# Listing the DeltaNet gates and first head pair first, and moving one S5 mixer behind DeltaNet, in a two-layer hybrid backbone on one core

## The chip, the cores and the metric

The kernel runs as one program on one core of a Trainium2 chip. The metric is the device time of one execution in microseconds (us), lower is better. The core's engines each work through their own list of instructions in a fixed order: TensorE (PE in the profile; PEld is its weight load, PEq its sequencer), VectorE (DVE), ScalarE (ACT), GpSimd (POOL), and SyncE (SP, which here issues nearly all transfers). An instruction waits for what it needs, and all that stands behind it on its engine waits with it. TensorE's clock has two levels, 1.2 and 2.4 GHz; the profile gives the granted clock of a stretch as a share of the upper one.

## The reference, cut to what matters

A flow-matching backbone of two layers over 768 tokens of width 1024: 256 context tokens and 512 latent ones. Only the latent tokens come out at the end, so in the second layer several stages handle those 512 alone. Each layer:

```
h  = modulated RMSNorm(x)
z  = h @ w_in        # dn_qkv, dn_z, dn_a, dn_b | s5_u | da_q, da_k, da_v | gla_...
y0 = gated DeltaNet(dn_qkv, dn_z, dn_a, dn_b)   # 4 heads of 64, both directions, chunks of 64
y1 = S5(s5_u)                                   # diagonal state space, width 256, both directions
y2 = differential attention(da_...)             # 4 heads
y3 = gated linear attention(gla_...)            # 4 heads
x  = x + w_out @ sum_i sigmoid(h @ w_gate_i + b_i) * (y_i @ w_branch_i)
x  = x + mixture of experts(modulated RMSNorm(x))    # 16 experts, top 2
```

DeltaNet cuts the tokens into chunks of 64; for each it solves a triangular system, and then carries a 64x64 state per head from chunk to chunk, one step after the other. `dn_a` and `dn_b` give its decay and its step size, the "gates" of this document's title; the sigmoids that weigh the four branches are called merge gates here.

## The kernel before, in words

Every large product runs as three matmuls of split operands: `wunit` loads a block of weights on SP, ScalarE makes the high part (L1318, L1315 with a scale), VectorE the low part (L1319, L1316), and `mm3` issues high x high, low x high and high x low on TensorE (L1328 to L1330). Blocks of weights pass through a small ring of buffers, so that the next loads wait until the splits before have read theirs.

In each layer `norm_a` writes the normalized tokens, and then one long function writes the four mixers in this order of the program text: projections, DeltaNet (`dn`, in the profile `dn_...`), gated linear attention (`gl_...`), differential attention (`da_...`), and the 32 blocks of merge gates (`pg`, L1735 to L1750), which need only the normalized tokens. `proj_cm` makes outputs with channels on the partitions (`pc`), `proj_tm` with tokens on them (`pt`). What a projection gives is stored to DRAM (`xd` for DeltaNet's q, k, v, `ud` for S5's input, `zd` for a gate of DeltaNet and also for a result within S5) and loaded again by its mixer.

A scheduler, not the text, sets the order on each engine: it walks the program with modelled durations and gives what is written earlier the preference. So the merge gates fill TensorE while the mixers wait. Pools bound this: DeltaNet's pool on the right side of SBUF is closed before S5's opens there when S5 follows, and DeltaNet's own has few buffers, so its second pair of heads runs behind its first. The pair loop stands at L1633; `dn_pair` is a generator that stops once, at `rq = next(pair)`, and is then run to its end. Names in the rows: `dn_n` norms of q and k, `dn_q`, `dn_u`, `dn_m`, `dn_b`, `dn_w`, `dn_o` the chunks' triangular solves and products, `dn_c` the state's steps (VectorE adds each to the state `Sh` at L640), `dn_s` the state's part of the outputs, `yT` the transposes of a mixer's result on its way to `yd`, `yst` the staged copy of it.

S5 (`s5_mix`) works in two halves of 128 channels: each loads tables (`td`, into `O`, `W`, `Tz`, `R`, `dec`) and its input `U` with a reversed copy `Ur`, makes `s_x` on TensorE, scans on VectorE, `s_y` on TensorE, and stores `z`; at the end `zT` and the weights `gw` are loaded, `s_g` makes a gate, and `ys` goes to `yd` (L1561). The tuple `S5E` says for each layer whether S5 is written ahead of DeltaNet or behind attention; before, the first layer has it behind and the second ahead, with its projection (columns from 1040) the first of all.

`merge` loads the four results from `yd` (`yr`, split into `yh`, `yl`), makes the branch products (`pb`), weighs and adds them on VectorE (L1787 to L1794), and multiplies by `w_out`, whose blocks are loaded through a ring of four.

Of the kernel before, what the change touches and what calls it, by code (L numbers as in the profile page):

```python
# [20 lines left out]
S5STEP = 4  # L21
NH = 4
DAST = 8
S5E = (0, 1)
AFTER = (1, 2, 5)
LP = (0, 0, 0)
PRP = (0, 0)
# [14 lines left out]
def const_blob():  # L42
# [21 lines left out]
    for n, a in parts.items():  # L64
# [11 lines left out]
PRO = {n: (sum(m for _, m in PRM[:i]), m) for i, (n, m) in enumerate(PRM)}  # L76
NPRM = sum(n for _, n in PRM)

WIN = ((1040, 256), (0, 256), (256, 256), (512, 256), (768, 272), (2832, 32), (2064, 256), (2320, 256), (2576, 256),
       (1552, 256), (1296, 256), (1808, 256))  # L80


def lay_out(x):
# [49 lines left out]
    o["wm"] = wm.reshape(2, 2, 4, 128, 24, 256).transpose(0, 4, 1, 3, 2, 5).reshape(2, 24, 2, 128, 1024)  # L133
    for c, n in WIN:
        o[f"win{c}"] = a["w_in"][:, :, c:c + n].reshape(2, 2, 4, 128, n).transpose(0, 1, 3, 2, 4).reshape(2, 2, 128, 4 * n)
# [209 lines left out]
def dn_conv(K, xp, m):  # L345


    nc, p, w = K.nc, K.dn, K.convw
    acc = p.tile([128, 772], F32, tag="s3", bufs=K.dn3, name="cacc")
    nc.scalar.activation(acc, xp[:, 0:772], AF.Copy, scale=w[:, 0, m:m + 1])  # L350
    for k in range(1, 5):
        nc.vector.scalar_tensor_tensor(acc, xp[:, k:k + 772], w[:, k, m:m + 1], acc, op0=OP.mult, op1=OP.add)
    th = p.tile([128, 772], F32, tag="s3", bufs=K.dn3, name="cth")
    nc.scalar.activation(th, acc, AF.Tanh, scale=0.5)
    nc.vector.scalar_tensor_tensor(acc, th, 1.0, acc, op0=OP.add, op1=OP.mult)
    return acc
# [294 lines left out]
def finish_heads(K, pool, tag, o, tiles, eps, gain, z=None, rq=None, sq=None, head=None):  # L651

    nc = K.nc
    t0, t1 = tiles
    n = (t1 - t0) * (o.shape[2] if head is None else 1)
    ov = o[:, t0:t1].rearrange("p t h e -> p (t h) e") if head is None else o[:, t0:t1, head]
    nc.scalar.activation(sq[:, 0:n, :], ov, AF.Square)
    ss = pool.tile([128, n], F32, tag=tag + "ss", name=tag + "ss")  # L660
    nc.vector.tensor_reduce(ss, sq[:, 0:n, :], axis=AX.X, op=OP.add)
    if rq is not None:
        rqv = rq[:, t0:t1].rearrange("p t h -> p (t h)")
        nc.vector.tensor_mul(ss, ss, rqv)
        nc.vector.tensor_mul(ss, ss, rqv)
    nc.vector.tensor_scalar(ss, ss, 1.0 / 64, eps, op0=OP.mult, op1=OP.add)
    r = rsqrt_(nc, pool, ss, [128, n], tag + "rs")
    if rq is not None:
        nc.vector.tensor_mul(r, r, rqv)
    nc.vector.tensor_mul(ov, ov, r[:, :, None].to_broadcast([128, n, 64]))  # L670
    gb = gain[:, None, :].to_broadcast([128, n, 64])
    if z is None:
        nc.vector.tensor_mul(ov, ov, gb)
        return
    zv = z[:, t0:t1].rearrange("p t (h e) -> p (t h) e", e=64)
    th = sq[:, 0:n, :]
    nc.scalar.activation(th, zv, AF.Tanh, scale=0.5)
    nc.vector.scalar_tensor_tensor(th, th, 1.0, zv, op0=OP.add, op1=OP.mult)
    nc.vector.tensor_mul(th, th, gb)
    nc.vector.tensor_mul(ov, ov, th)  # L680
# [642 lines left out]
def mm3(nc, out, terms, n=None):  # L1323


    n = n or len(terms)
    for i, (ah, al, bh, bl) in enumerate(terms):
        nc.tensor.matmul(out, ah, bh, start=(i == 0), stop=False)  # L1328
        nc.tensor.matmul(out, ah, bl, start=False, stop=False)  # L1329
        nc.tensor.matmul(out, al, bh, start=False, stop=(i == n - 1))  # L1330
# [120 lines left out]
def proj_units(K, ring, w, c0, n):  # L1451

    out = []
    for h in range(2):
        hi, lo = wunit(K, ring, K.I[f"win{c0}"][w, h].rearrange("p (k n) -> p k n", k=4), [128, 4, n], 3)
        out += [(hi[:, k], lo[:, k]) for k in range(4)]
    return out


def proj_cm(K, ring, w, ah, al, c0, n, parts, sink):  # L1460

    nc = K.nc
    u = proj_units(K, ring, w, c0, n)
    for m in range(0, n, 128):
        r = min(128, n - m)
        for s0, s1 in parts:
            ps = K.psd("pc")
            mm3(nc, ps[0:r, 0:s1 - s0], [(u[k][0][:, m:m + r], u[k][1][:, m:m + r], ah[:, k, s0:s1], al[:, k, s0:s1]) for k in range(8)])
            sink(m // 128, r, ps, (s0, s1))


def proj_tm(K, ring, w, ah, al, c0, n, tiles, sink):

    nc = K.nc
    u = proj_units(K, ring, w, c0, n)
    for t in tiles:
        ps = K.psd("pt")
        c = slice(t * 128, t * 128 + 128)
        mm3(nc, ps[:, 0:n], [(ah[:, k, c], al[:, k, c], u[k][0], u[k][1]) for k in range(8)])
        sink(t, ps)  # L1480


def put_yT(K, o, nch, tiles, yd, new, psm):

    nc = K.nc
    t0, t1 = tiles
    for j in range(nch):
        st = new([128, 768], "yst")
        a = t0
        while a < t1:  # L1490
            b = min(a + 4, t1)
            ps = psm("yT")
            for t in range(a, b):
                nc.tensor.transpose(ps[:, (t - a) * 128:(t - a + 1) * 128], o(t, j), K.c("id"))
            nc.scalar.activation(st[:, a * 128:b * 128], ps[:, 0:(b - a) * 128], AF.Copy)
            a = b
        nc.sync.dma_start(yd[j][:, t0 * 128:t1 * 128], st[:, t0 * 128:t1 * 128])
# [9 lines left out]
def s5_tds(K, l):  # L1507
    return [K.dram.tile([128, 7680], F32, name=f"td{l}{h}") for h in range(2)]


def mixers(K, l, md, hold, tile_of, yd, gd, tds):
# [7 lines left out]
    full = [(0, 256), (256, 768)]  # L1519
# [9 lines left out]
    ah = pa.tile([128, 8, T], F32R, name="ah")  # L1529
    al = pa.tile([128, 8, T], F32R, name="al")  # L1530
# [5 lines left out]
    w = l  # L1536
# [4 lines left out]
    ring = Hold(tc, f"pring{l}", "left")  # L1541
# [8 lines left out]
    def stage(shape, nm):  # L1550
        return ring.tile(shape, F32, tag="st" + str(shape[1]), bufs=2, name=nm)
# [11 lines left out]

    if S5E[l]:
        proj_cm(K, ring, w, ah, al, 1040, 256, full, sink_u)
# [4 lines left out]
    def sink_xd(base):  # L1570
        st = {}

        def f(m, r, ps, s):
            if s[0] == 0:
                st[0] = stage([128, 776], "xst")
                nc.gpsimd.memset(st[0][:, 0:2], 0.0)
                nc.gpsimd.memset(st[0][:, 258:262], 0.0)
                nc.gpsimd.memset(st[0][:, 774:776], 0.0)
            o = 2 if s[0] == 0 else 6
            nc.scalar.activation(st[0][:, s[0] + o:s[1] + o], ps[:, 0:s[1] - s[0]], AF.Copy)  # L1580
            if s[1] == T:
                nc.sync.dma_start(xd[m + base], st[0])
        return f

    for b in range(3):
        proj_cm(K, ring, w, ah, al, 256 * b, 256, full, sink_xd(2 * b))
    ab = gring.tile([128, NT, 16], F32, name="ab")

    def sink_z(t, ps):
# [4 lines left out]
            nc.sync.dma_start(zd[t * 128:(t + 1) * 128], st[:, 0:256])  # L1594

    proj_tm(K, ring, w, ah, al, 768, 272, range(NT), sink_z)
    if l == 0:
        st = Hold(tc, "s5t0", "right")
        tds = s5_tds(K, 0)
        for _ in s5_build(K, 0, st, K.psmb, tds, 4, 2):  # L1600
            pass
        st.close()
# [4 lines left out]
    if l == 0:  # L1607
# [3 lines left out]
        def some(n):  # L1611
            for _ in range(n):
                i, u = next(todo)
                mods(K, i, md[i], [u], pm, MB, K.psmb)
# [10 lines left out]
    def convs(pr):  # L1625
        tl = []
        for m in (pr, 2 + pr, 4 + pr):
            xp = dn.tile([128, 776], F32, tag="s3", bufs=K.dn3, name="xp")
            nc.sync.dma_start(xp, xd[m])
            tl.append(dn_conv(K, xp, m))  # L1630
        return tl

    for pr in range(2):  # L1633
        if pr and l == 0:
            some(MODS[1])
        ya = dn.tile([128, NT, 2, 64], F32, tag="ya", name="ya")
        pair = dn_pair(K, l, pr, S, *(tl if pr else convs(0)), ya, need)
        rq = next(pair)
        if pr == 0:
            tl = convs(1)  # L1640
        for _ in pair:
            pass
        zt = dn.tile([128, NT, 128], F32, tag="s3", bufs=K.dn3, name="zt")
        nc.sync.dma_start(zt[:, T0:], zd[T0 * 128:, 128 * pr:128 * pr + 128].rearrange("(t p) c -> p t c", p=128))
        finish_heads(K, dn, "fa", ya, (T0, NT), 1e-6, gain, zt, rq, sq=dn.tile([128, NT * 2, 64], F32, tag="s3", bufs=K.dn3, name="fsq"))
        put_yT(K, lambda t, j: ya[:, t].rearrange("p h e -> p (h e)"), 1, (T0, NT), yd[0, pr:pr + 1],
               lambda sh, n: dn.tile(sh, F32, tag="s3", bufs=K.dn3, name=n), K.psm)
# [21 lines left out]
    with tc.high_priority(PRP[l]):  # L1669
# [7 lines left out]
        proj_tm(K, ring, w, ah, al, 1808, 256, range(NT), sink_tm(vd, 0, 256))  # L1677
        if not S5E[l]:
            proj_cm(K, ring, w, ah, al, 1040, 256, full, sink_u)
# [51 lines left out]

    if not S5E[l]:
        s5()
# [770 lines left out]
```

## Time and profile before

| | |
|---|---|
| runs | 2712.81, 2721.1, 2722.15 us, median 2721.1 |
| profiled execution | 2708.16 us, its span 2706.4 us |
| TensorE busy, matmul | 2381.9 us, 88% of the span |
| TensorE busy, weight load | 1919.3 us, 71% |
| VectorE busy | 1894.2 us, 70% |
| ScalarE busy | 1228.0 us, 45% |
| GpSimd busy | 201.4 us, 7% |
| mean granted TensorE clock | 0.92 |

The shares are means over stages of different kinds: the mixers, where TensorE has projections and merge gates to fill it; the end of the mixers in each layer, where it has not; the merge; and the experts. Times in the rows are microseconds from the span's start. A busy time of a group of rows counts overlapping instructions once, while a mean duration is that of a single one, so that the count times the mean can exceed the busy time: matmuls are pipelined.

### The profile page before, as it was taken

The page shows a single profiled execution, that of the slowest core. Times are in us where ns is not written, and L with a number is a line of the kernel's source. Part 1 is how long each engine was busy: PE and PEld are TensorE (multiplying, and loading weights), DVE is VectorE, ACT ScalarE, POOL GpSimd, SP SyncE. Part 2 cuts the span into 40 slices and gives each one's busy share as a digit, 9 for nine tenths or more (in the row PEclk, how much of TensorE's full clock was granted, in tenths as well). Part 3 has the DMA queues.
Part 4 walks back from the last instruction along what each step waited for, and adds up shares of the span by engine and source line. Part 5 has one row for each costly group of instructions (what it writes and reads, how often), then busy time and mean ns, then how long its engine had stood idle before and what let it go on. Part 6 is the DMA issues. An engine that isn't in the chain of part 4 may idle for free. (4 is left out here: it accounts for less than half of the span.)

```text
span 2706.4 us, 46025 instructions
## 1 busy us (share of the span) xinstructions
PE 2381.9 (88%) x17551; PEld 1919.3 (71%) x17551; DVE 1894.2 (70%) x3917; ACT 1228.0 (45%) x1933; POOL 201.4 (7%) x220
## 2 busy tenths in 40 slices
PE   6999999999987894988989399999998877699993
PEld 4887668878865773776767288987786556588872
DVE  5857767864564957896778654677676586787785
ACT  4232233455533212655656332343666442476672
POOL 0000000000000000221221000000000000132210
PEclk8999999999986996999999699999997589799997
DMA  7488753431523764776778654443341085698884
GB/s 291 151 303 275 240 181 96 152 95 59 175 77 128 236 225 159 287 275 246 275 270 292 248 169 137 132 134 125 122 132 49 7 281 205 232 379 300 316 297 155
DMA packets 233719, 534.96 MB, mean 198 GB/s; under 512 B 86054, under 2 KB 116486, under 8 KB 207878
## 3 DMA queue, kind: packets, MB, share of 16 engines
q1 hardware_dynamic: 222534, 510.83, 55.2%
q0 software_dynamic: 10944, 20.99, 2.2%
q8 instruction: 142, 2.33, 0.3%
q14 instruction: 99, 0.81, 0.1%
HBM read 452.34 MB, written 100.35 MB: 204 GB/s over the span
## 5 line engine op out<-in xcount | busy, mean ns | idle before, releaser
L2228 DVE TENSOR_TENSOR lo<-raw,hi 128x2048 fp32r<-128x2048 f32 x192 | 437.8, 2289 | 87.7 <-ACT hi L2226 86.2
L2226 ACT ACTIVATE hi<-raw 128x2048 fp32r<-128x2048 f32 x192 | 364.6, 1914 | 100.5 <-PE pg L1330 71.8
L1328 PE MATMUL pg<-ah,wh 128*128 128x512 f32 (+1 forms) x768 | 280.2, 365 | 4.2 <-ACT gst L1748 4.0
L1330 PE MATMUL pg<-ah,wl 128*128 128x512 f32 (+1 forms) x768 | 280.0, 365 | 0.7 <-DVE wl L1319 0.7
L1329 PE MATMUL pg<-al,wh 128*128 128x512 f32 (+1 forms) x768 | 279.8, 364 | 0.0
L1329 PE MATMUL pg<-lo,xh 128*128 128x512 f32 x608 | 246.9, 407 | 12.6 <-DVE lo L2228 12.5
L1328 PE MATMUL pg<-hi,xh 128*128 128x512 f32 x608 | 243.9, 406 | 12.5 <-ACT hi L2226 11.9
L1319 DVE TENSOR_TENSOR wl<-wr,wh 128x512 fp32r<-128x512 f32 (+3 forms) x208 | 164.9, 795 | 118.9 <-ACT wh L1318 113.6
L1330 PE MATMUL pg<-hi,xl 128*128 128x512 f32 x608 | 244.1, 403 | 0.0
L1318 ACT ACTIVATE wh<-wr 128x512 fp32r<-128x512 f32 (+3 forms) x208 | 148.0, 715 | 211.4 <-PE pg L1329 83.7
L1328 PEld LDWEIGHTS pg<-ah,wh 128*128 128x128 f32 x768 | 147.5, 192 | 29.6 <-ACT gst L1748 5.0
L1330 PEld LDWEIGHTS pg<-ah,wl 128*128 128x128 f32 x768 | 147.4, 192 | 23.9 <-issue 1.9
L1329 PEld LDWEIGHTS pg<-al,wh 128*128 128x128 f32 x768 | 147.3, 192 | 22.1 <-issue 1.8
L1328 PE MATMUL pt<-wh,ah 128*128 128x256 f32 (+1 forms) x544 | 156.6, 289 | 2.1 <-ACT zst L1593 2.1
L1329 PE MATMUL pt<-wl,ah 128*128 128x256 f32 (+1 forms) x544 | 156.9, 289 | 0.0
L1330 PE MATMUL pt<-wh,al 128*128 128x256 f32 (+1 forms) x544 | 156.7, 288 | 0.0
L1329 PEld LDWEIGHTS pg<-lo,xh 128*128 128x128 f32 x608 | 117.6, 193 | 42.7 <-DVE lo L2228 19.0
L1328 PEld LDWEIGHTS pg<-hi,xh 128*128 128x128 f32 x608 | 116.9, 193 | 39.2 <-ACT hi L2226 14.7
L1330 PEld LDWEIGHTS pg<-hi,xl 128*128 128x128 f32 x608 | 117.1, 193 | 22.7
L1328 PE MATMUL pd<-hi,hh 128*128 128x512 f32 x304 | 120.1, 395 | 4.9 <-ACT hh L2280 4.9
L1328 PE MATMUL pc<-ah,wh 128*128 128x512 f32 (+3 forms) x352 | 120.4, 343 | 0.8 <-ACT ust L1556 0.7
L1329 PE MATMUL pc<-al,wh 128*128 128x256 f32 (+3 forms) x352 | 120.6, 343 | 0.0
(727 smaller groups left out, 5340.9 us busy)
## 6 DMA issues: line engine op xcount, KB each, us to landing
raw<-in_w_e_gate SPq DMA_DIRECT2D x64, 1024.0 KB
raw<-in_w_e_up SPq DMA_DIRECT2D x64, 1024.0 KB
raw<-in_w_e_down SPq DMA_DIRECT2D x64, 1024.0 KB
w<-in_wm SPq DMA_DIRECT2D x80, 512.0 KB
wr<-in_w_gate SPq DMA_DIRECT2D x128, 256.0 KB
wr<-in_win SPq DMA_DIRECT2D x40, 512.0 KB
gd<-gst SPq DMA_DIRECT2D x32, 384.0 KB
g<-gd SPq DMA_DIRECT2D x32, 384.0 KB
```

The lines of the kernel that those rows point to most:

```text
L1318: nc.scalar.activation(h, r, AF.Copy)
L1319: nc.vector.tensor_sub(l, r, h.bitcast(F32))
L1328: nc.tensor.matmul(out, ah, bh, start=(i == 0), stop=False)
L1329: nc.tensor.matmul(out, ah, bl, start=False, stop=False)
L1330: nc.tensor.matmul(out, al, bh, start=False, stop=(i == n - 1))
L2226: nc.scalar.activation(h, r, AF.Copy)
L2228: nc.vector.tensor_sub(l_, r, h.bitcast(F32))
```

## The change

Two things are changed. The tuple `S5E` puts the second layer's S5, with the projection of its input, behind DeltaNet and attention in the program text, as in the first layer. And among DeltaNet's projections the one with `dn_z`, `dn_a`, `dn_b` (columns 768 to 1040) comes first, followed by three blocks of 128 columns for the first pair of heads; the second pair's three blocks of 128 are written inside the pair loop, after the first pair's generator has stopped for the first time. Before, three blocks of 256 columns made q, k and v for both pairs at once, and `dn_z`, `dn_a`, `dn_b` followed. `WIN` lists the blocks in which the host lays out the weights. Both layers have the new order of projections.

```diff
-S5E = (0, 1)
+S5E = (0, 0)
...
-WIN = ((1040, 256), (0, 256), (256, 256), (512, 256), (768, 272), (2832, 32), (2064, 256), (2320, 256), (2576, 256),
+WIN = ((768, 272), (0, 128), (256, 128), (512, 128), (128, 128), (384, 128), (640, 128), (1040, 256), (2832, 32), (2064, 256), (2320, 256), (2576, 256),
        (1552, 256), (1296, 256), (1808, 256))
...
-    for b in range(3):
-        proj_cm(K, ring, w, ah, al, 256 * b, 256, full, sink_xd(2 * b))
+    def proj_pair(pr):
+        for b in range(3):
+            proj_cm(K, ring, w, ah, al, 256 * b + 128 * pr, 128, full, sink_xd(2 * b + pr))
+
     ab = gring.tile([128, NT, 16], F32, name="ab")
...
     proj_tm(K, ring, w, ah, al, 768, 272, range(NT), sink_z)
+    proj_pair(0)
     if l == 0:
...
         rq = next(pair)
         if pr == 0:
+            proj_pair(1)
             tl = convs(1)
```

The first place is the end of the second layer's mixers on TensorE, from the last merge-gate matmul on. This is the order before; `da_...` is attention, `dn_q` the start of the second pair's triangular solves.

```order
L1330 MATMUL pg<-ah,wl 128x512
L928 MATMUL da_o<-V,pe 64x64 x8
L864 MATMUL da_t<-idr,sp 96x128 x6
L918 MATMUL da_s<-st 128x512 x2
L864 MATMUL da_t<-idr,sp 96x128 x4
L918 MATMUL da_s<-st 128x512 x2
L864 MATMUL da_t<-idr,sp 96x128 x2
L928 MATMUL da_o<-V,pe 64x64 x8
L864 MATMUL da_t<-idr,sp 96x128 x4
L918 MATMUL da_s<-st 128x512 x2
L877 MATMUL da_m<-st 128x384
L508 MATMUL dn_q<-A,L 32x32
```

And this is the order of the changed kernel from its last merge-gate matmul on.

```order
L1330 MATMUL pg<-ah,wl 128x512
L877 MATMUL da_m<-st 128x384
L637 MATMUL dn_c<-Sh,Mt 64x64 x4
L877 MATMUL da_m<-st 128x384 x2
L928 MATMUL da_o<-V,pe 64x64 x8
L637 MATMUL dn_c<-Sh,Mt 64x64 x4
L877 MATMUL da_m<-st 128x384
L918 MATMUL da_s<-st 128x512
L637 MATMUL dn_c<-Sh,Mt 64x64 x4
L918 MATMUL da_s<-st 128x512
L637 MATMUL dn_c<-Sh,Mt 64x64 x2
L877 MATMUL da_m<-st 128x384
```

The second pair's solves moved ahead of the last merge gate; of its 40 state matmuls 28 stand behind it, four to a chunk. S5's first matmuls of the second layer follow them, among attention:

```order
L928 MATMUL da_o<-V,pe 64x64 x8
L877 MATMUL da_m<-st 128x384 x3
L928 MATMUL da_o<-V,pe 64x64 x8
L877 MATMUL da_m<-st 128x384
L918 MATMUL da_s<-st 128x512
L1198 MATMUL s_x<-U,W_22659 64x96 x12
L918 MATMUL da_s<-st 128x512
L1198 MATMUL s_x<-U,W_22659 64x96 x4
L877 MATMUL da_m<-st 128x384 x2
L1198 MATMUL s_x<-Ur,W_22661 64x96 x8
```

All of S5's matmuls in this layer now stand behind the last merge gate; before, all of them stood ahead of it, among the projections.

The second place is SP's list at the same end. Before, DeltaNet's and attention's last stores, the first six loads of `w_out` and the results' reloading for the merge:

```order
L1497 DMA yd_17483<-yst 128x512
L595 DMA EG<-gd 64x1024 x2
L1497 DMA yd_17483<-yst 128x512
L1310 DMA wr<-in_w_out 128x512 x4
L1497 DMA yd_17483<-yst 128x512
L1310 DMA wr<-in_w_out 128x512 x2
L1310 DMA yr<-yd_17483 128x512 x4
L1310 DMA wr<-in_w_branch 128x512 x2
```

In the changed kernel, from the first load of `w_out`, right behind attention's last store, to the same reloading:

```order
L1310 DMA wr<-in_w_out 128x512 x5
L1265 DMA zT<-zd 128x512
L1310 DMA wr<-in_w_out 128x512 x4
L1250 DMA zd<-z_22974 16x8x64 x8
L1310 DMA wr<-in_w_out 128x512 x2
L1265 DMA zT<-zd 128x512
L1267 DMA gw<-in_s_glu_w 128x2x256
L1310 DMA wr<-in_w_out 128x512 x5
L1561 DMA yd_17519<-ys_23095 128x512
L1561 DMA yd_17519<-ys_23107 128x512
L1310 DMA yr<-yd_17519 128x512 x4
L1310 DMA wr<-in_w_branch 128x512 x2
```

All sixteen loads of `w_out` moved ahead of S5's last stores and so of the merge; ten of them stood within the merge before.

## Rows read from the trace of the kernel before

**Rows 1.** Table by stretches: start:end, length, busy us (x instructions), clock, DMA share, GB/s.
```profile
core 0: us, PE busy (x) PEld busy (x) DVE busy (x) ACT busy (x) POOL busy (x), PEclk, DMA share, GB/s
...
791.00:857.00 66.00, 46.93 (x389) 31.97 (x388) 34.13 (x98) 17.80 (x38) 0.32 (x3) 0.61 0.14 41
1550.00:2041.00 491.00, 483.31 (x4095) 411.27 (x4093) 323.94 (x727) 213.20 (x405) 12.03 (x32) 0.99 0.44 133
2041.00:2166.00 125.00, 105.39 (x1211) 75.21 (x1210) 75.54 (x222) 66.27 (x158) 0.84 (x4) 0.63 0.11 28
...
2178.00:2234.00 56.00, 51.02 (x192) 35.40 (x192) 53.52 (x89) 22.18 (x36) 0.00 (x0) 0.97 0.83 277
```

**Rows 2.** Tiles dn_n and pg, TensorE, second layer: durations ns min/median/max, first, last start.
```profile
L382 PE MATMUL dn_n<-sq,cb x48: 272/273/297, 1715.1 to 1966.1; 128*32 128x128 f32 x48
...
L1330 PE MATMUL pg<-ah,wl x256: 387/389/632, 1779.2 to 2040.8; 128*128 128x512 f32 x128
```

**Rows 3.** Groups of TensorE, 1550 to 1690: S5's first and last of five.
```profile
L1239 PE MATMUL s_y<-X,O 64*64 64x64 f32 x256 | 10.9, 226 | 0.0
...
L1198 PE MATMUL s_x<-Ur,W 128*64 128x96 f32 x64 | 3.1, 249 | 0.0
```

**Rows 4.** The same view, 1690 to 1960, first pair: state matmuls; eight other groups' first, third, last.
```profile
L637 PE MATMUL dn_c<-Sh,Mt 64*64 64x64 f32 x80 | 6.0, 230 | 0.0
L540 PE MATMUL dn_u<-KR,Tt 64*64 64x64 f32 x96 | 3.8, 222 | 0.0
...
L568 PE MATMUL dn_m<-kd,W 64*64 64x64 f32 x80 | 3.3, 225 | 3.3 <-DVE Mt L570 3.3
...
L516 PE MATMUL dn_q<-Tt,Q 32*32 32x32 f32 x96 | 1.0, 193 | 0.0
```

**Rows 5.** Time line of VectorE, 2131 to 2167: first and last of ten state updates.
```profile
2133.13 0.60 DVE L640 TENSOR_TENSOR Sh<-Sh,dn_c 64x128 f32<-64x128 f32 x2
...
2153.90 0.59 DVE L640 TENSOR_TENSOR Sh<-Sh,dn_c 64x128 f32<-64x128 f32 x2
```

**Rows 6.** Time line of TensorE, 2164.5 to 2179: start, us, instruction, [idle before <-releaser].
```profile
2165.21 1.09 PE L1494 MATMUL yT<-cb,ya 128*128 128x128 f32 x4 [3.05 <-DVE ya L680]
2177.76 0.80 PE L1328 MATMUL pb<-yh,wh 128*128 128x512 f32 x1 [11.46 <-ACT wh L1318]
```

**Rows 7.** Time lines of TensorE: DeltaNet's last transposes, S5's halves, first and second layer.
```profile
712.35 0.82 PE L1494 MATMUL yT<-cb,ya 128*128 128x128 f32 x6
...
734.35 0.88 PE L1198 MATMUL s_x<-U,W 128*64 128x96 f32 x16
...
791.75 1.54 PE L1198 MATMUL s_x<-U,W 128*64 128x96 f32 x32
...
1595.74 0.96 PE L1198 MATMUL s_x<-U,W 128*64 128x96 f32 x18
...
1636.58 1.54 PE L1198 MATMUL s_x<-U,W 128*64 128x96 f32 x32 [0.52 <-DMA U<-ud]
```

**Rows 8.** Time lines of SP's queue: S5's stores in both layers, its first input load.
```profile
850.57 3.72 SPq L1561 DMA_DIRECT2D yd<-ys  x2
...
1581.22 0.46 SPq L1185 DMA_DIRECT2D U<-ud  x1
...
1684.41 0.32 SPq L1561 DMA_DIRECT2D yd<-ys  x1
```

**Rows 9.** Groups of VectorE, 2178 to 2234: the splits of w_out.
```profile
L1316 DVE SCALAR_TENSOR_TENSOR wl<-wr,wh 128x512 fp32r<-128x512 f32 x10 | 6.8, 696 | 0.0
```

**Rows 10.** Waits, 1550 to 2041: waited for, us in total, times, longest.
```profile
ACT wh L1318 <- DMA wr<-in_w_gate: 25.8, 10, 8.0
```

**Rows 11.** Groups of TensorE, 2041 to 2166.5: attention's matmuls on V and scores.
```profile
L918 PE MATMUL da_s<-st 98*128 98x512 f32 x34 | 20.4, 644 | 2.1 <-ACT st L865 1.7 <-ACT pe L921 0.4
...
L928 PE MATMUL da_o<-V,pe 128*64 128x64 f32 x288 | 17.5, 289 | 1.4 <-DVE pe L924 1.3
```

## The prediction

> **What bounds the kernel now.** I began with the table of stretches [rows 1], which cuts the second layer where its character changes. From 1550 to 2041 us TensorE is busy 483.3 of 491 us at full clock: there the kernel lasts as long as TensorE's queue, and no wait of another engine shows in the time. It ends with the last gate matmul: the row of the gate tile has its last start at 2040.8 [rows 2]. From 2041 to 2166 the same engine is busy 105 of 125 us at a granted clock of 0.63, between the levels 1.2 and 2.4 GHz: what is left there is a chain, DeltaNet's second pair of heads, with attention's remainder beside it. Third, the merge, 2178 to 2234: VectorE 53.5 and TensorE 51.0 of 56 us, so VectorE is just ahead.
>
> Who ends the tail is in the time lines: DeltaNet's ten state updates on VectorE run from 2133.13 to 2153.90 [rows 5], its normalized result is transposed at 2165.21, and the merge's first matmul starts 12.6 us later, at 2177.76, held by the split of a stored result [rows 6]. The second pair starts late because its first norm matmuls stand behind the first pair's: the norm tile's 48 matmuls run in two bursts, from 1715.1 and at 1966.1 [rows 2]. S5 of this layer was done long before, its last store issued at 1684.41 [rows 8].
>
> So the change is read as an exchange: S5's chain goes from a stretch that TensorE fills anyway to the end of the layer's chain, and DeltaNet's second pair goes the other way.
>
> **Term 1: TensorE's queue up to the last gate matmul, +5 us.** S5's five groups of matmuls leave it; busy times 10.9 to 3.1 us, sum 26.4 [rows 3]. By the order, all of the second pair but 28 of its 40 state matmuls now stands ahead of the last gate matmul. At full clock the first pair shows what that is worth: eight groups, 3.8 to 1.0 us, sum 21.6, and 12/40 of the state matmuls' 6.0, 1.8 [rows 4]. Of attention, 16 of 136 instructions on V and 6 of 34 score matmuls come ahead too: 16/136 x 17.5 + 6/34 x 20.4 = 5.7 us in the tail [rows 11], at full clock about 5.7 x 0.63 = 3.6. So 27.0 comes for 26.4. To this I add one wait of the size that the first pair has, 3.3 us on VectorE before `dn_m` [rows 4], and a microsecond for smaller ones. Bounds: 0, and +14 for four such waits.
>
> **Term 2: the tail, +17 us.** What stands behind the last gate matmul has four links, one after the other.
> The seven remaining state updates: ten took 20.8 us [rows 5], about 2.1 each, so 15 (13 for six intervals, 20 if they take as long as all ten).
> From the last update to the transposes of DeltaNet's result: 2165.21 - 2153.90 = 11.3 [rows 5, 6].
> From there to S5's first matmul: S5's buffers open only when DeltaNet's are closed, and its tables and `U` are loaded then. The first layer, which already has this order, shows it: 712.35 to 734.35, 22.0 us [rows 7]. The second layer of before shows 14.5 us from the issue of the first `U` (1581.22) to its first matmul (1595.74) [rows 7, 8], a floor. I take 20, since less is on the DMA queues in the tail than among the first layer's gate loads.
> S5 from its first matmul to its last store: 1684.41 - 1595.74 = 88.7 us at full clock, 120 in the first layer (734.35 to 850.57 + 3.72), where the second half ran at the tail clock [rows 7, 8]. The first half takes 40.8 before the second starts (1636.58), and the second 47.8 in the second layer, 62.5 in the first [rows 7, 8]. With attention beside it and no gates, I take 41 + 55 = 96.
> Sum 15 + 11 + 20 + 96 = 142; before, the same way is 2165.2 - 2041 = 124 to 125. The 12.6 us from there to the merge's first matmul stay: S5's store is loaded and split as DeltaNet's was. Bounds: 13 + 11 + 14.5 + 88.7 = 127 (+2) and 20 + 11 + 22 + 120 = 173 (+48).
>
> **Term 3: the merge, -4 us.** Ten splits of `w_out` lie in its first stage, 6.8 us of VectorE [rows 9]. In the new order they stand ahead of S5's last outputs, so they are done in the tail, beside a chain that leaves VectorE time (75.5 of 125 busy [rows 1]). TensorE's 51.0 is then next; of the 56 us about 4 can go. Bounds 0 (the splits delay S5's output by as much) and -6.8.
>
> **Term 4: projections and the first layer, 0.** Matmuls are the same in number and length; six loads and splits of 512 KB become twelve of 256 KB. They are hidden behind TensorE's queue: ScalarE waited 25.8 us, ten times, for gate weights of 256 KB [rows 10], in a stretch in which TensorE lost 7.7 us to everything [rows 1]. If the cover were gone, at the start of a layer's projections, each load would show its latency, some 2.6 us by that row. The earlier start of DeltaNet is nothing in itself, since the queue is what lasts. In the first layer the order barely changes but at one place: S5's second half stood right behind the last gate matmul (it started at 791.75 [rows 7]) and now some 45 gate matmuls stand behind its start, half of them of half length; at 0.39 us [rows 2] for the long ones that is up to 12 us of head start. But what feeds that half (tables, `U`) comes when it came before, so I take nothing. Bounds -12 and +8 (three loads uncovered).
>
> A rule speaks against the smaller loads. The Trainium skill, DMA: Bandwidth & Descriptors, section Bandwidth, asks for loads of 1 MiB and more, and gives 0.95 us for 64 KB and 6.15 for 1 MB; between these lines, an estimate, twelve loads of 256 KB are 23.9 us and six of 512 KB 20.3, +3.6 us a layer, which would make the time below about 7 us longer. No run here times one load by itself; the row of the gate weights lets me keep 0.
>
> **Sum.** 5 + 17 - 4 + 0 = +18 us on the profiled execution's own 2708.2, 2726. That execution lies 12.9 us under the median of the runs, 2721.1, so I forecast 2739 us. A measurement here can tell about 0.5%, 13.6 us, from no change.
>
> **The rivals.**
> No measurable change: every link of the tail at its floor, 127 us, because TensorE stays at the 2.4 GHz level, as it was in S5 of before. Then +2 +2 -4 = 0, up to +13: 2721 to 2734. For it: nothing of S5 needs more than the 88.7 shown. Against: the tail's clock was 0.63 with as many of attention's wide matmuls in it as there will be, and the first layer's S5 tail (791 to 857) has 0.61 [rows 1]. The halves can't run side by side to win it back: in TensorE's new order all of the first half's output matmuls stand ahead of the second half's first.
> Faster: the place is the first layer's S5. If its second half really starts 12 us before the last gate matmul, the 66 us of that layer's tail [rows 1] become 54. It decides only if the second layer's tail also stays at its floor: +2 +2 -4 -12 = -12, and with the whole 6.8 us of the merge -15, 2706 to 2709; any term of the second layer above its floor takes it back. For it: a queue that is freed there is worth its full length, since TensorE waits in that tail. Against: of the first layer's 57 us between the halves nothing shows TensorE's queue as the cause.
> Slower by more: on SP eleven `w_out` loads now stand between the first `zT` and S5's own stores; the ring has four buffers, each freed by a VectorE split, and what is queued behind a waiting load is S5's result, for which the merge waits. Six splits of 0.7 us and loads between them are some 8 us; with S5 at the first layer's 120 us the tail is 15 + 11 + 20 + 120 + 8 = 174, +49, and in all 2766 to 2775.
> The change may also leave DeltaNet where it was: if the second pair still ended last, the tail would hold both chains. The order excludes this, but not waits in the gates' stretch (Term 1's upper end).
>
> **Chances and range.** Forecast, slower by 0.5 to 1.5%: 0.39. Slower by more: 0.14. No measurable change: 0.31. Faster by over 0.5%, for this rival and what I don't see: 0.16. That makes 0.53 slower, 0.31 same, 0.16 faster. For 8 in 10 the range leaves out most of the faster case and half of the worst: 2704 to 2772. The likeliest case alone lies from 2735 to 2762.
>
> **What would show it.** The new profile should have: the last gate matmul within 0 to 14 us of 2041, measured from the layer's start; the first pair's norm matmuls some 90 us earlier and the second's over 100; the last state update some 15 us behind the last gate matmul, instead of 113; S5's first matmul some 46 us behind it; S5's last store as the last release before the merge; no `w_out` split among the merge's first products; the first layer's tail as long as before. I am wrong if S5 takes under 89 us in the tail, if the tail's clock is near 1, or if the gate stretch grows by more than 14 us because DeltaNet's waits now stand in TensorE's queue.

## The result, and the profile after

The changed kernel takes 2736.3 us in the median of four runs (2731.6 to 2739.3), the kernel before 2719.0; the ratio is 1.0065, 95% interval 1.0041 to 1.0089: slower, as forecast, by 17 us where 18 were worked out. Run again later it gave 1.0065 (1.0036 to 1.0095). The profiled execution took 2731.6 us, its span 2729.8, 23.4 more than that of before.

The table of stretches of the changed kernel (columns as in [rows 1]). The rows of the second layer are cut at the same events as before, but the second one, the tail, runs on to S5's last store; the first row's start, 781, is no event: it lies 4 us ahead of the start of S5's second half and 15 ahead of the first layer's last gate matmul.

```profile
core 0: us, PE busy (x) PEld busy (x) DVE busy (x) ACT busy (x) POOL busy (x), PEclk, DMA share, GB/s
...
781.00:848.00 67.00, 56.23 (x460) 40.37 (x459) 35.74 (x103) 21.05 (x48) 0.25 (x2) 0.70 0.19 56
1540.00:2044.00 504.00, 494.67 (x4406) 419.33 (x4406) 312.10 (x700) 225.23 (x432) 12.06 (x30) 0.98 0.39 114
2044.00:2197.00 153.00, 102.04 (x901) 74.18 (x899) 96.24 (x271) 65.75 (x155) 0.82 (x6) 0.55 0.33 102
...
2206.00:2256.00 50.00, 48.03 (x191) 36.31 (x189) 46.26 (x76) 15.37 (x25) 0.00 (x0) 0.95 0.76 242
```

Against [rows 1]: the stretch that TensorE fills is 504 instead of 491 us, the tail 153 instead of 125, and at a granted clock of 0.55 instead of 0.63; the merge's products are shorter, and there TensorE, with 48.0 of 50, is now ahead of VectorE.

The tiles `dn_n` and `pg` (answering to [rows 2]) show what moved: the second layer starts at 1539.9 now, 9.7 us earlier; relative to that the first pair's norms start 93 us earlier, and the second pair's last one starts 129 us earlier, while the last gate matmul comes 12.6 us later.

```profile
L382 PE MATMUL dn_n<-sq,cb x48: 272/273/297, 1612.4 to 1827.0; 128*32 128x128 f32 x48
...
L1330 PE MATMUL pg<-ah,wl x256: 387/389/796, 1770.5 to 2043.7; 128*128 128x512 f32 x128
```

The tail's chain on TensorE, from the time line (answering to [rows 6, 7]): DeltaNet's transposes, the starts of S5's two halves, S5's gate, and the merge's first product.

```profile
2072.70 1.09 PE L1494 MATMUL yT<-cb,ya 128*128 128x128 f32 x4 [8.68 <-DVE nx L895]
...
2092.11 2.19 PE L1198 MATMUL s_x<-U,W 128*64 128x96 f32 x24 [0.28 <-issue]
...
2143.84 2.51 PE L1198 MATMUL s_x<-U,W 128*64 128x96 f32 x28 [1.02 <-DMA U<-ud]
...
2188.38 6.20 PE L1277 MATMUL s_g<-zT,gw 128*128 128x256 f32 x16 [15.43 <-DMA gw<-in_s_glu_w]
2204.98 0.80 PE L1328 MATMUL pb<-yh,wh 128*128 128x512 f32 x1 [10.41 <-ACT wh L1318]
```

And the end of it on SP's queue (answering to [rows 8]): the loads of `w_out` stand between S5's `zT`, its second half's stores of `z`, `gw` and its own last stores.

```profile
2173.59 0.43 SPq L1265 DMA_DIRECT2D zT<-zd  x1
2174.57 3.59 SPq L1310 DMA_DIRECT2D wr<-in_w_out  x4
2178.21 3.81 SPq L1250 DMA_DIRECT2D zd<-z  x8
...
2183.86 0.43 SPq L1267 DMA_DIRECT2D gw<-in_s_glu_w  x1
2184.33 6.29 SPq L1310 DMA_DIRECT2D wr<-in_w_out  x5
2194.00 2.76 SPq L1561 DMA_DIRECT2D yd<-ys  x2
```

The span's 23.4 us are made up so: -9.7 up to the second layer's first norm matmul; +12.6 from there to the last gate matmul; +24.3 from that to the merge's first product (137.0 before, 161.3 now); -4.4 from there to its second product (56.2, 51.8); +0.6 after it.

### The profile page after: what moved, and what is told of

It reads as the page before. It is cut to its first block, busy times and chain, and to the rows that moved or that the text cites. A ratio compares the mean times of both kernels' runs of the same rounds, so it can differ in the third digit from the quotient of the medians.

```text
span 2729.8 us, 46084 instructions
## 1 busy us (share of the span) xinstructions
PE 2380.6 (87%) x17551; PEld 1925.5 (71%) x17551; DVE 1897.2 (69%) x3929; ACT 1231.1 (45%) x1945; POOL 196.2 (7%) x220
## 5 line engine op out<-in xcount | busy, mean ns | idle before, releaser
L1328 PE MATMUL pc<-ah,wh 128*128 128x256 f32 (+3 forms) x352 | 120.3, 343 | 2.2 <-ACT qst L1669 1.2
```

## The experiments

"S5 late" and "S5 early" mean the second layer's S5 behind or ahead of DeltaNet. The times of all kernels, with the ratio to the kernel before on the same chip. The kernels ran on several chips, so two medians of different rows can belong to different chips; the ratio, over all runs and with its interval, is the safer comparison. The last column is from one profile of each kernel.

| kernel | median us | ratio (95%) | from the second layer's start to its last gate matmul, to the merge's first product, to its second product |
|---|---|---|---|
| before | 2715 to 2719 | 1 | 491.2, 137.0, 56.2 |
| the change | 2736.3 | 1.0065 (1.0041 to 1.0089) | 503.8, 161.3, 51.8 |
| the change again | 2737.3 | 1.0065 (1.0036 to 1.0095) | 503.0, 162.4, 51.5 |
| S5 late alone | 2734.5 | 1.0072 (1.0045 to 1.0098) | 485.4, 172.3, 51.7 |
| projections alone | 2716.6 | 1.0005 (0.9978 to 1.0032) | 507.1, 142.0, 56.1 |
| gates first, whole blocks | 2692.9 | 0.9908 (0.9877 to 0.9939) | 500.5, 120.3, 63.0 |
| the same again | 2692.9 | 0.9909 (0.9875 to 0.9943) | 496.1, 119.1, 64.7 |
| gates first, whole, S5 late | 2715.1 | 0.9998 (0.9973 to 1.0022) | 500.4, 154.0, 50.7 |
| split in the second layer only | 2700.3 | 0.9932 (0.9909 to 0.9956) | 505.3, 120.3, 64.9 |
| split, all in front | 2734.8 | 1.0065 (1.0035 to 1.0095) | 497.1, 121.3, 62.4 |
| the change, `w_out` late | 2742.4 | 1.0092 (1.0058 to 1.0126) | 506.4, 156.3, 59.8 |
| the change, no attention | 2667.3 | 0.9826 (0.9759 to 0.9894) | 465.5, 138.2, 51.8 |
| the change, 6 gate blocks held | 2712.6 | 1.0005 (0.9975 to 1.0035) | see below |
| gates first, whole, S5 late, 6 held | 2699.9 | 0.9953 (0.9928 to 0.9977) | see below |

**S5 late alone.**

```diff
 # the kernel before
-S5E = (0, 1)
+S5E = (0, 0)
```

> The kernel before with S5E = (0, 0) alone: the second layer's S5 behind DeltaNet, projections as before. Theory (the two halves of the change act in different layers: the S5 move costs the second layer some 33 us between its start and its second product, the new projection order gives the first layer 9.7): first layer as before (S5's second half at 791 to 793, merge at 867 to 868), second layer slower than in the changed kernel, because more of the second pair (12 dn_b, all dn_w, dn_o and 40 dn_c instead of 28 dn_c) stands behind the last merge gate: 30 to 42 us over the kernel before, ratio 1.011 to 1.016. Rival (the new projections cost the second layer time, and the S5 move little): within 10 us of before, ratio under 1.004.

It is 17 us slower than before, as slow as the whole change. The rival falls, but the size of the theory does too, 30 to 42 us: the tail is longer than the change's, as expected (172.3), and the stretch ahead of it shorter (485.4), since there is less of the second pair in it. The merge, with the `w_out` splits out of it, gives 4.5 us back (51.7).

**Projections alone.**

```diff
 # the changed kernel
-S5E = (0, 0)
+S5E = (0, 1)
```

> The changed kernel with S5E = (0, 1): the new projection order in both layers, the second layer's S5 ahead of DeltaNet as before. Theory: the first layer keeps its 9 to 10 us, the second layer's end is as before (the order has the same second-pair instructions behind the last merge gate), so 5 to 13 us faster than before, ratio 0.995 to 0.998. Rival (the 12 smaller loads uncover latency in the second layer's start): second layer 5 us or more slower than before from its first norm matmul to its last merge gate, ratio 0.999 or more.

No change that can be measured. The first layer's merge starts at 856.1, 11.4 us earlier than before, so the theory's gain is there, but the second layer takes it back: 507.1 to the last gate matmul, and 142.0 behind it. The rival's number was met, but not its reason: in those 507.1 us TensorE is idle for 7.1, against 7.7 in [rows 1], so no load's latency shows there. What differs is the granted clock, 0.95 against 0.99.

**Gates first, whole blocks.**

```diff
 # the kernel before
-    for b in range(3):
-        proj_cm(K, ring, w, ah, al, 256 * b, 256, full, sink_xd(2 * b))
...
     proj_tm(K, ring, w, ah, al, 768, 272, range(NT), sink_z)
+    for b in range(3):
+        proj_cm(K, ring, w, ah, al, 256 * b, 256, full, sink_xd(2 * b))
```

> The kernel before with one thing changed: the projection of the gates (768 to 1040) ahead of the three blocks of 256, which stay whole. S5E as before. Theory (the first layer gains because DeltaNet starts some 5 us earlier and S5's second half comes to stand ahead of the last merge gates): the first layer's S5 store 6 to 10 us earlier, ratio 0.995 to 0.998. Rival (the gain comes from listing the second pair's blocks later): first layer within 3 us of before, ratio 0.999 to 1.001.

More than expected: 25 us faster than before, and the same in a second set of runs. Its second layer's tail has the same matmuls as that of projections alone, in another order. VectorE's time line shows it, first and last state update of the second pair, in projections alone (last gate matmul at 2045.6):

```profile
2140.64 0.60 DVE L640 TENSOR_TENSOR Sh<-Sh,dn_c 64x128 f32<-64x128 f32 x2
...
2163.14 0.59 DVE L640 TENSOR_TENSOR Sh<-Sh,dn_c 64x128 f32<-64x128 f32 x2 [0.69 <-PE dn_c L637]
```

and in the second profile of gates first (last gate matmul at 2039.2), where then TensorE's time line shows the end of the mixers:

```profile
2111.15 0.60 DVE L640 TENSOR_TENSOR Sh<-Sh,dn_c 64x128 f32<-64x128 f32 x2 [2.18 <-PE dn_c L637]
...
2127.47 0.29 DVE L640 TENSOR_TENSOR Sh<-Sh,dn_c 64x128 f32<-64x128 f32 x1
```

```profile
2144.05 1.05 PE L1494 MATMUL yT<-cb,ya 128*128 128x128 f32 x4
...
2157.59 1.09 PE L1494 MATMUL yT<-cb,o 128*128 128x128 f32 x4 [10.87 <-DVE o L673]
2158.32 0.78 PE L1328 MATMUL pb<-yh,wh 128*128 128x512 f32 x1
```

Here the scheduler put the last 28 state matmuls together, ahead of attention's remainder. DeltaNet's result is transposed 13 us before attention's last, the loads of five of the eight stored results are issued meanwhile, and its first product stands 0.7 us behind attention's transposes, where [rows 6] has 12.6 behind DeltaNet's. The merge then takes longer, 63 to 65 us, as its later inputs come in (the last three stored results are loaded from 2161.38 on); in all some 10 us are won from the last gate matmul to the second product (183 to 184 against 193.2).

**Gates first again.** The same kernel.

> The gates-first kernel once more, beside the others on one chip, for a second profile. Theory: 2688 to 2703, ratio 0.988 to 0.994; last merge gate to the merge's second product near 183 us, first layer's merge at 848 to 857. Rival (its gain was that chip's): ratio above 0.996.

It repeats: 183.8 us from the last gate matmul to the second product, the first layer's merge at 849.1.

**Gates first, whole blocks, S5 late.**

```diff
 # gates first, whole blocks
-S5E = (0, 1)
+S5E = (0, 0)
```

> The gates-first kernel (whole blocks of 256, gates ahead of them) with the second layer's S5 moved behind DeltaNet: the change without the splitting into pairs. Theory (the S5 move is what costs, by a longer chain behind the last merge gate, whatever the projection order): 18 to 30 us slower than the gates-first kernel (ratio 0.991 to the kernel before), so 2708 to 2724 us, ratio 0.998 to 1.003; last merge gate to the merge's first product 155 to 172 us. Rival (splitting the pairs is what costs, and the S5 move is cheap on this base): within 8 us of the gates-first kernel, ratio 0.989 to 0.994.

22 us slower than gates first with S5 early: the theory's band; the way to the merge's first product, 154.0, is just below its 155. So in the medians moving S5 costs 17 (old projections: 2734.5 against 2717.5), 20 (new ones: 2736.3 against 2716.6) or 22 us, on three bases; by the ratios it is 0.7, 0.6 and 0.9%, or 20, 16 and 24 us. With intervals of some 0.3% on each ratio the three do not differ.

**Split in the second layer only.**

```diff
 # projections alone
+    if l:
         proj_pair(0)
+    else:
+        for b in range(3):
+            proj_cm(K, ring, w, ah, al, 256 * b, 256, full, sink_xd(2 * b))
...
-            proj_pair(1)
+            if l:
+                proj_pair(1)
```

> S5 early as before; gates first in both layers; the blocks of 256 whole in the first layer, and split into pairs with the second pair's listed midway in the second layer alone. By the order this kernel's second layer ends as the gates-first kernel's does (the last 28 state matmuls of the second pair stand together, ahead of attention's remainder), where the projections-only kernel has them spread among attention as before. Theory (splitting costs nothing by itself; the 24 us between the projections-only and the gates-first kernel are the order that the scheduler gives the tail, 15 us, and the first layer, 8 us): within 8 us of the gates-first kernel, 2688 to 2703, ratio 0.989 to 0.994, last merge gate to the merge's second product 175 to 190 us. Rival (smaller loads and the later listing cost in the second layer's queue): 12 us or more over the gates-first kernel, ratio 0.995 or more.

The theory's band: 7 us over gates first, which the intervals of the two do not separate, and 185.2 us from the last gate matmul to the second product. (Blocks of both widths are laid out for it.) The text of the second layer is that of projections alone; only the first layer's differs, and with it the scheduler's order in the second layer's tail. So of the 24 us between projections alone and gates first most is the first layer's text and the order that the tail got with it, not the smaller loads in the second layer: in the profiles the first layer's merge starts 7 us earlier than in projections alone (848.7 against 856.1), and the tail up to the second product is 13 us shorter (185.2 against 198.1).

**Split, all in front.**

```diff
 # projections alone
     proj_pair(0)
+    proj_pair(1)
...
-            proj_pair(1)
```

> S5 early as before; gates first; blocks of 128 in both layers, first pair's then second pair's, all six listed in front, nothing midway. By the order its second layer ends as the gates-first kernel's; its first layer has S5's first half later, 148 of its output matmuls behind the last merge gate instead of 68. Theory (time follows the order of the two tails, not the block size): second layer from its first norm matmul to the merge's second product within 8 us of the gates-first kernel's 684, first layer's tail 10 to 25 us longer, so 2698 to 2720. Rival (block size costs): second layer 10 us or more over 684.

The second layer is as the theory has it, 497.1 + 121.3 + 62.4 = 680.8, between the 683.8 and 679.9 of the two profiles of gates first: here the smaller loads cost the second layer nothing that shows. The total misses the expected 2698 to 2720. The first layer is far worse than expected: its last gate matmul is over at 788.5, and its merge starts at 891.9, 103 us later; before this was 76. By the order, 148 of S5's output matmuls and half of its first ones stand behind that gate. The direction was read from the order, the size was not.

**The change, `w_out` late.**

```diff
 # the changed kernel; raw_ring: the pool of the raw buffers
     wo = [[wunit(K, pw, I["w_out"][l][...],
-                 [128, 1, 512], 16, WOUT[l], scale=0.5) for n in range(2)] for k in range(8)]
+                 [128, 1, 512], 16, WOUT[l], scale=0.5, raw_tag="wor" if l else None, raw_ring=pr if l else None)
+           for n in range(2)] for k in range(8)]
```

> The changed kernel with the raw buffers of the second layer's w_out taken from the merge's own pool, which opens behind S5: the 16 loads no longer stand ahead of S5's stores on SP. Theory (they hold S5's last stores and the wait for gw back by some 4 us, and are worth 4 us in the merge): from S5's last output matmul to its last store 3 to 6 us less, the merge's first product 3 to 5 us longer, in all within 4 us of the changed kernel, ratio to the kernel before 1.005 to 1.008. Rival (the loads are the main part of the tail's excess over the forecast): 6 to 10 us faster than the changed kernel, ratio 1.003 or less.

Both parts were seen: S5 from first matmul to last store 100.0 us instead of 104.3, the merge 59.8 instead of 51.8. From the last gate matmul to the second product that is a loss of 3 us in the profile. The ratio, 1.0092, lies above the expected 1.005 to 1.008, though its interval overlaps that of the change. The loads on SP are 4 us of S5's time, all in its second half (48.3 instead of 52.6, while the first half stays at 51.7), and are worth nearly twice as much in the merge.

**The change, no attention in the second layer.**

```diff
 # the changed kernel
+    if l == 0:
         with tc.high_priority(PRI[l]):
             diff_attn(K, l, qk, V, o, l == 0, done)
+    else:
+        nc.vector.memset(o, 0.0)
+        ... # the two put_yT of the zeros
```

> The changed kernel without the second layer's attention (its output is set to zero before the transposes, so its matmuls, exponentials and vector work are left out there). It asks what attention's remainder costs the tail. Theory (the chain of DeltaNet's last steps and S5 sets the tail, attention stretches it only by what it puts ahead on the engines): last merge gate to S5's last store 125 to 140 us instead of 152, S5 from first matmul to last store 88 to 97 instead of 104. Rival (the tail lasts as long as its engines are shared with attention, half of it is attention's work): S5 under 80 us, tail under 115.

Its stretch from the last gate matmul to S5's last store:

```profile
2007.60:2137.40 129.80, 47.66 (x557) 38.77 (x556) 57.65 (x129) 19.30 (x36) 0.82 (x6) 0.57 0.37 116
```

129.8 us, in the theory's band; S5 alone, from 2052.27 to its last store's issue at 2137.36, takes 85.1, less than that band, at a granted clock of 0.58. In the stretch TensorE is busy 48 us, so for 82 us of it TensorE waits for a chain. The edit moves one more thing: the sixteen loads of `w_out` are issued here between 2009 and 2027, ahead of S5's first matmul, so S5's stretch is without attention and without them. What the two are worth apart has to be read from the halves of S5, as is done below.

**The change, six gate blocks held for the tail.**

```diff
 # the changed kernel
+    hold = Hold(tc, "hold", "right") if l else None
     if not S5E[l]:
         s5()
...
-                hi, lo = wunit(K, gring, I["w_gate"][l, j, h].rearrange("p (k n) -> p k n", k=4),
-                               [128, 4, 128], 3)
+                late = l and j >= 32 - NHOLD      # NHOLD = 6
+                hi, lo = wunit(K, hold if late else gring, I["w_gate"][l, j, h].rearrange("p (k n) -> p k n", k=4),
+                               [128, 4, 128], 2 if late else 3)
```

> The changed kernel with the last 6 of the second layer's 32 merge-gate blocks loaded through buffers of a pool that opens when DeltaNet's closes, so that they run in the tail, between S5's steps. All work is kept. Theory (in the tail TensorE waits, so work that fills the stretch before is free there): 6 blocks at 24 x 0.233 us are 33 us less before the tail, and the tail grows by 5 to 15, its clock above 0.7; 15 to 30 us faster than the changed kernel, ratio to the kernel before 0.995 to 1.001. Rival (the tail's engines are shared so closely that added matmuls lengthen S5's chain as much): within 8 us of the changed kernel, ratio 1.004 to 1.009.

Faster than the change by 24 us in the medians, 16 by the ratios (1.0005 against 1.0065); it is level with the kernel before. From the second layer's start to the merge's second product it takes 695.7 instead of 716.9. The stretch up to S5's last store, where the held gates are:

```profile
2017.50:2174.00 156.50, 122.94 (x1083) 90.17 (x1081) 100.33 (x281) 76.48 (x176) 0.72 (x5) 0.78 0.39 121
```

TensorE is busy 123 us of 156.5, at a granted clock of 0.78 (0.87 from S5's first matmul to its last store), and S5 takes 104.6 instead of 104.3: here the dense work put into the waits of the chain cost the chain nothing that shows.

**Both.** The same edit on gates first, whole blocks, S5 late.

> Gates first with whole blocks, S5 late in the second layer, and the last 6 merge-gate blocks held for the tail: the two gains together. Theory: the gates-first order's gain and the held gates' gain add, 2685 to 2702 us, ratio 0.987 to 0.994, faster than the kernel before, about equal to or faster than gates first alone. Rival: held gates give nothing, 2708 to 2724, as the same kernel without them.

2699.9 us, 15 us less than the same kernel without held blocks, so the gains add in part. It beats the kernel before (0.9953, above the expected 0.987 to 0.994), but not gates first with S5 early. Here the held blocks were not free for the chain: S5 takes 107.7 us, against 102.4 without them.

**The change again.** The same kernel.

> The changed kernel once more, for a second profile. Theory: the links of the second layer's tail repeat within 3 us (last merge gate to DeltaNet's transposes 29, from there to S5's first matmul 19, S5 104, then 8.6 to the merge), while the stretches in which TensorE is full vary by up to 10 us with the granted clock. Rival (the tail varies as much): links off by more than 5 us.

The links repeat: 31.0 from the last gate matmul to DeltaNet's transposes (29.7 in the first profile, both to the last of the four), 19.7 from there to S5's first matmul (18.7), S5 104.0 (104.3), then 7.7 (8.6). The stretch before was 503.0 (503.8).

## Why the prediction was right, by its own steps

**Term 1**, +5, measured +12.6 in the two profiles, inside its bounds. The waits that I added, 4.3 us, were not it: TensorE's busy time rose from 483.3 [rows 1] to 494.7, and its idle time only from 7.7 to 9.3. Part of that is attention, whose four groups `da_m`, `da_s`, `da_o` and `da_t` sum to 33.8 us there instead of 26.0, where I had counted 3.6 more and only `da_o` and `da_s`; part may be the clock, 0.98 against 0.99. How much is the change's own stays open: the second profile of the change has 503.0, but projections alone, with S5 early, has 507.1 in this stretch at a clock of 0.95, so a single pair of profiles does not measure this term to better than some 10 us.

**Term 2**, +17, measured +24.3, is one step that was too small, with Term 1. By links: to DeltaNet's transposes 29 (26 forecast), from there to S5's first matmul 19 (20), S5 104 (96); the way to the merge was 4 us shorter than the 12.6 I kept. The state updates behind the last gate matmul ran as forecast: in the time line of VectorE the last one starts at 2057.44, 14 us behind it. The mis-sized term is S5, and within it the first half. I had carried that half over from the kernel before, 41 us, and lengthened only the second, to 55; measured are 51.7 (2092.11 to 2143.84) and 52.6. The first half before, in the change, and without attention (columns as in [rows 1]):

```profile
1595.74:1636.58 40.84, 40.33 (x394) 34.47 (x394) 20.67 (x39) 6.93 (x15) 0.57 (x8) 1.00 0.50 165
...
2092.11:2143.84 51.73, 41.41 (x371) 28.80 (x372) 32.76 (x95) 21.29 (x54) 0.23 (x2) 0.53 0.29 85
...
2052.27:2092.47 40.20, 16.13 (x224) 13.17 (x225) 17.17 (x37) 2.47 (x7) 0.22 (x2) 0.58 0.36 113
```

Without attention the half has its 41 us again, at a clock of 0.58, so attention makes the difference (the `w_out` loads stand in this half in neither kernel), and VectorE is where it shows: from S5's first step on that engine to its last `X`, 24.6 us in the change (2093.84 to 2118.48), 14.8 without attention (2054.49 to 2069.32), with attention's row maxima (`nm`, L878) between S5's steps. The other late kernels lie in line: S5 late alone, with 27.0 us of VectorE work in the half, takes 47.5, gates first with S5 late, with 29.9, takes 49.2. The second half is 7.7 us longer than without attention; the `w_out` loads, which stand in it and are worth 4.3 there by the kernel with `w_out` late, explain more than half of that.

The reason that I gave for the lengthening, the tail's lower clock, is not shown. S5's matmuls do take longer at it: `s_y` 323 ns without attention instead of 226 [rows 3], all five groups 40.6 us instead of 26.4.

```profile
L1239 PE MATMUL s_y<-X,O 64*64 64x64 f32 x256 | 17.3, 323 | 9.2 <-DVE X L1226 9.1
```

But S5 as a whole takes 85.1 at 0.58 without attention and 88.7 before at full clock [rows 7, 8], where TensorE was busy for 88.1 of those 88.7 us and only 26.4 of them were S5's. What the clock costs the chain and what the queue of projections cost it before may cancel; no run parts the two.

**Term 3**, -4, measured -4.4 and -4.6, with the cause that was named: no `w_out` split is left among the merge's first products, and with the loads put back it is 59.8.

**Term 4**, 0 for the projections, is right in the sum and by cancelling. Gates first is worth 25 us with S5 early and 19 with S5 late; splitting gives 24 and 21 back. Neither shows in the way that I looked at, loads and their latency; with S5 early both go with the orders that the scheduler gives the tails, and with S5 late no run asks. In the first layer what I had set aside as a rival's mechanism happened in part: S5's second half starts at 784.6 instead of 791.75 [rows 7], gate matmuls stand behind it until 796.4, and the layer's merge starts 9.5 us earlier, so the sign that the first layer's tail would be as long as before failed. The second layer then starts 9.7 us earlier; in the second profile the merge starts 6.2 us earlier and the second layer 2.6.

**The sum.** In the two profiles: +12.6 + 24.3 - 4.4 - 9.7 + 0.6 = 23.4; in the medians 17 to 19. The direction and the mechanism, a chain moved to the end, are borne out: S5's move alone is worth 17 to 22 us, the projections nothing. That 18 was met so closely is luck: Terms 1 and 2 were 7 to 8 us too small each, the first layer gave 9.7 back, and the profiled execution of before lies 11 us under the median of its runs where that of the change lies 5 under.

**The rivals.** "No measurable change" needed the tail at 127 and TensorE at its upper level, and failed: the tail's clock is 0.55, and S5 is at its floor only without attention and the `w_out` loads. (In that rival's sum, +2 for Term 1 has no row behind it.) "Slower by more" named SP's queue; the `w_out` loads cost 4 us there, not 8. "Faster" had its mechanism in the first layer, and the second layer took it back, as its condition said. The Trainium skill's rule on small loads (DMA: Bandwidth & Descriptors, section Bandwidth), from which 3.6 us a layer was estimated, has its table for loads issued from GpSimd, while these are issued from SP. It does not show in the second layer: TensorE's idle time there is 7.1 us with the smaller loads (projections alone) and 7.7 before, and the layer took 680.8 us up to its second product with them (split, all in front) and 683.8 and 679.9 without (gates first, twice). It is not refuted: no run times the loads by themselves, and differences of 4 us are within what two profiles of one kernel differ by.

## What to carry to other kernels

Moving a serial mixer from a stretch that fills TensorE to the end of the chain costs about what it lengthens that chain, less what leaves it; count the links behind the last filler instruction, and count the other work that shares their engines as part of each link: here attention, mostly by its work on VectorE, made 11 us of S5's first half. When a chain must stand alone at the end, hold back some of the filler for it: six blocks of merge gates kept for the tail won back some 20 us (16 by the ratios, 24 in the medians), and cost the chain nothing that shows in one kernel and 5 us in the other. And where a scheduler sets the order, read the order of the tail after every edit, also one far away: here an edit to the first layer's text made 13 us of difference at the end of the second.

## What the runs showed of the hardware that was not expected

The spread between runs of one kernel goes with the granted clock: of 29 runs of the kernel before on one chip, the shortest took 2698 us at a mean clock of 0.930, the longest 2735 at 0.910. The profiled execution of before (2708.2, 0.920) is shorter than each of its own runs, which is part of why its gate stretch looks short beside the others. In four profiles with nearly the same matmuls in it, that stretch was 491.2 us at a clock of 0.99 (before), 496.1 at 0.98 and 500.5 at 0.97 (gates first, twice) and 507.1 at 0.95 (projections alone). TensorE's idle time in it is 7 to 9 us in all four; whether the kernels' own work pulls the clock down there is not shown.

What a chain of small matmuls feels of the clock is less plain than its matmuls suggest: S5's five groups took 26.4 us with TensorE at full clock and 40.6 at 0.58, its steps on VectorE in the first half 14.8 us at either, and S5 as a whole 88.7 beside projections at full clock, 85.1 with nothing beside it at 0.58, and 104.3 and 104.6 beside attention at 0.55 and 0.87, the last with the held gates there too.
